# A decoder layer on one core: weight splits on GpSimd, fewer indexer columns, a fixed order in the merge, and the overflow branch at the end

## The chip, the cores and the metric

The kernel runs on one core of a Trainium2 chip. The metric is the device time of one execution in microseconds (us); the median of several executions is compared. The engines are TensorE (PE; its weight loads are PEld), VectorE (DVE), ScalarE (ACT), GpSimd (POOL) and SyncE (SP, which here only issues transfers).

## What is computed

One decoder layer for 512 tokens of width 1024, in float32, and a final RMSNorm:

```python
h = rms_norm(x, g_mix)
qa, ka, va, qb, kb, vb, qi, ki, wi, ga, gb = jnp.split(h @ w_in, SPLIT_POINTS, axis=-1)
qa, ka, qb, kb, qi, ki = (rope(t) for t in (qa, ka, qb, kb, qi, ki))
o_a = moba_attend(qa, ka, va)       # causal blocks
o_b = dsa_attend(qb, kb, vb, qi, ki, wi * IDX_SCALE)   # top 128 keys by the indexer's scores
mixed = sigmoid(ga) * (o_a @ w_proj_a) + sigmoid(gb) * (o_b @ w_proj_b)
x = x + mixed @ w_out
x = x + hier_moe(rms_norm(x, g_ffn), ...)   # top group of 4, top 2 of its 8 SwiGLU experts
return rms_norm(x, g_final)
```

A token attends at most 128 keys in branch B, so the first 128 tokens need no selection and the indexer's scores are only taken for tokens 128 to 511.

## The kernel before

A product of float32 precision is made of three matmuls in a faster type: a matrix is split into a high part (a cast on ScalarE, L172) and a low part (raw minus high, L173, on VectorE or GpSimd), and high times high, high times low and low times high are summed (L266 to L268).

**First part, to about 460 us.** The input projection comes in chunks of 256 columns. SyncE loads each chunk in two halves into one of three buffers `raw`; `halves_of` splits the first half on VectorE and the second on GpSimd into `wh` and `wl`, of which there are two each. `two_blocks` multiplies a chunk in two blocks of 128 columns, 8 steps of 3 matmuls each, over all 512 tokens. `rope_of` rotates on VectorE; `q_stack` and `k_stack` copy the result on ScalarE and take low parts on GpSimd (L319 `qi`, `qa`; L330 `loka`; `kst` is the indexer's key, L384). The indexer's scores (L400 to L404) go into `bias`; the attention quads a0, a1, b0, b1 (scores L443, softmax result `e` L450) are interleaved with the projections by a table of shares (`SHARE`), so that TensorE has other matmuls while a softmax runs. TensorE's instructions are in the order of the program; the other engines are ordered by a scheduler, in which the chunks have a high priority.

**The merge.** For each of 8 blocks of 128 columns TensorE multiplies branch B's output with its projection (12 matmuls, L514 to L516) into one of three PSUM banks `mm`; VectorE multiplies with the gate (L650) and adds branch A (L651); ScalarE writes the high part of the sum for the four token blocks (`mt`, L654), VectorE the low part (L655). The bank is free after that. Between them lie the splits of w_out, three on GpSimd and the last on VectorE. Then x2 = x + mixed W_out (L685 to L689), the norm, the router and a one-hot gather with 32 slots for each expert.

**Second part, from about 480 us.** The 32 experts come in 8 groups of four (`q`), each of 24 pieces of 1 MB that SyncE fetches (L619) into buffers as these come free; TensorE multiplies (L868, L875) and scatters back by a one-hot product into x (L932 to L935). Every token of an expert beyond its 32nd is handled by `rest_of_tokens`, under an If on the largest count. The inputs here have none, so the branch is not entered. The If stands before group 6 (`REST`): eight pieces (`BRIDGE`) are issued by ScalarE ahead of it, then come the load of the count (L1027) and the branch (L1028).

**The tail.** In the last group, for each of 4 token blocks, the first half of x is finished by `combine`, squared on ScalarE (L1088) and multiplied by the norm's weight; then the second half the same way, GpSimd's add and power give the norm's factor (L1105, L1106), the halves are scaled on ScalarE and VectorE (L1107, L1109), and each is sent off by a transfer of 256 KB.

## Time and profile before

| | before |
|---|---|
| median of 3 runs (lowest, highest) | 937.04 us (935.4, 939.02) |
| profiled execution | 939.58 us, its span 937.5 us |
| mean granted clock of TensorE | 0.984 |
| busy: TensorE, VectorE, ScalarE, GpSimd | 93%, 45%, 30%, 19% |

The shares of busy time are averages over two parts of a different kind. The rate of the transfers, slice by slice, tells them apart; then each wait is read in its own stretch: which engine stands, and for whom. The granted clock is given as a share of 2.4 GHz: 1.00 is that, 0.50 is 1.2 GHz.

### The profile page before, as it was taken

How to read it: one execution, taken by the hardware profiler on the slowest of the kernel's cores; microseconds unless marked ns; L12 is line 12 of the kernel's file. 1: busy time of each engine (PE TensorE's matmuls, PEld its weight loads, DVE VectorE, ACT ScalarE, POOL GpSimd, SP SyncE). 2: the span in 40 equal slices, each digit the busy share in tenths (PEclk: the TensorE clock that was granted, in tenths of full speed). 3: DMA queues.
4: the chain of work that ended last, by engine and by line, in shares of the span. 5: the costliest groups of instructions: out<-in, count | busy, mean ns of one | idle time of the engine just before them, and what ended most of it. 6: DMA issues, size and time to landing. Idle time of an engine off the chain costs nothing. (4 is left out here: it accounts for less than half of the span.)

```text
span 937.5 us, 15635 instructions
## 1 busy us (share of the span) xinstructions
PE 875.8 (93%) x6436; PEld 518.0 (55%) x6436; DVE 426.5 (45%) x981; ACT 278.5 (30%) x585; POOL 178.6 (19%) x115
## 2 busy tenths in 40 slices
PE   7999989989999999899999999999998989599885
PEld 5897769768777877689834343422423223133221
DVE  3747899998545554641722323231421302313114
ACT  4546654553443554533510100010100100001013
POOL 1494335243114820600300000000000000000003
PEclk9999999999999999899999999999999999799998
DMA  8422112112214221574589999999999999989995
GB/s 324 153 81 68 46 46 91 45 45 91 68 68 180 90 91 50 188 289 180 208 359 420 420 420 421 420 419 420 419 421 420 421 420 419 417 330 418 422 419 201
DMA packets 41261, 244.49 MB, mean 261 GB/s; under 512 B 4961, under 2 KB 5345, under 8 KB 16609
## 3 DMA queue, kind: packets, MB, share of 16 engines
...
## 5 line engine op out<-in xcount | busy, mean ns | idle before, releaser
L868 PE MATMUL h<-we,xs 128*32 128x512 f32 x2048 | 237.4, 600 | 25.9 <-DMA we<-in_w_e_dram 16.7
L868 PEld LDWEIGHTS h<-we,xs 128*32 128x32 f32 x2048 | 59.0, 110 | 179.3 <-issue 111.9
L875 PE MATMUL y<-we,hT 128*32 128x512 f32 x1024 | 116.1, 595 | 3.0 <-DMA we<-in_w_e_dram 3.0
L266 PE MATMUL mm<-xh,wh 128*128 128x512 f32 x272 | 110.2, 405 | 0.8 <-DVE bias L404 0.8
L268 PE MATMUL mm<-xh,wl 128*128 128x512 f32 x272 | 107.7, 396 | 0.0
L267 PE MATMUL mm<-xl,wh 128*128 128x512 f32 x272 | 107.7, 396 | 0.0
L173 POOL TENSOR_TENSOR wl<-raw,wh 128x1024 fp32r<-128x1024 f32 (+1 forms) x23 | 64.4, 2801 | 135.0 <-ACT wh L172 76.9
L1094 POOL TENSOR_TENSOR fo<-x,gfn 128x512 f32<-128x512 f32 x4 | 5.0, 1272 | 446.4 <-DVE x L935 446.4
L935 DVE TENSOR_TENSOR x<-cps,x 128x512 f32<-128x512 f32 x64 | 43.3, 688 | 82.0 <-PE cps L933 81.9
L875 PEld LDWEIGHTS y<-we,hT 128*32 128x32 f32 x1024 | 30.1, 109 | 74.5 <-issue 56.7
L909 DVE SCALAR_TENSOR_TENSOR silu<-silu,gate,h 128x512 f32<-128x512 f32 x16 | 12.0, 748 | 114.7 <-PE h L868 113.7
L268 PEld LDWEIGHTS mm<-xh,wl 128*128 128x128 f32 x272 | 51.2, 188 | 12.4
L266 PEld LDWEIGHTS mm<-xh,wh 128*128 128x128 f32 x272 | 51.4, 189 | 11.8 <-issue 1.2
L267 PEld LDWEIGHTS mm<-xl,wh 128*128 128x128 f32 x272 | 51.3, 189 | 9.6
L172 ACT CAST wh<-raw 128x1024 fp32r<-128x1024 f32 (+1 forms) x46 | 45.6, 1028 | 32.2 <-DMA raw<-in_w_ch_dram 13.2
L903 ACT ACTIVATE silu<-h 128x512 f32<-128x512 f32 x16 | 9.6, 598 | 146.7 <-PE h L868 119.2
L172 ACT CAST y<-y 128x512 fp32r<-128x512 f32 x32 | 18.7, 586 | 113.6 <-PE y L875 113.6
L916 ACT COPY hT<-htr 128x512 f32<-128x512 f32 x16 | 8.7, 588 | 147.3 <-PE htr L914 147.3
L173 DVE TENSOR_TENSOR y<-y,y 128x512 fp32r<-128x512 f32 x32 | 22.0, 688 | 54.3 <-ACT y L172 54.3
L448 ACT ACTIVATE ps<-e,st 128x128 f32<-128x128 f32 (+3 forms) x64 | 33.5, 524 | 43.7 <-DVE st L447 43.5
L173 DVE TENSOR_TENSOR wl<-raw,wh 128x1024 fp32r<-128x1024 f32 (+1 forms) x23 | 31.9, 1386 | 27.2 <-ACT wh L172 22.6
L687 PE MATMUL mm<-woh,mt 128*128 128x256 f32 x128 | 36.5, 285 | 1.2 <-DVE mt L655 1.2
(201 smaller groups left out, 1569.2 us busy)
## 6 DMA issues: line engine op xcount, KB each, us to landing
we<-in_w_e_dram SPq DMA_DIRECT2D x184, 1024.0 KB, 19.8
...
```

The source lines that it names most:

```text
L172: act.copy(hi, raw)
L173: eng.tensor_tensor(lo, raw, hi.bitcast(F32), ALU.subtract)
L266: pe.matmul(ps, a, xk(k, 0), start=k == 0, stop=False)
L267: pe.matmul(ps, a, xk(k, 1), start=False, stop=False)
L268: pe.matmul(ps, lo[:, k, col:col + P], xk(k, 0), start=False, stop=k == NK - 1)
L448: act.activation(ps[:, :n], e[:, :n], AF.Exp, bias=st[:, 0:1], scale=-1.0, accum_out=st[:, 1:2])
L687: pe.matmul(ps, mt[t][:, 1, k], hi[:, k], start=False, stop=k == NK - 1)
L868: pe.matmul(ps[h][CAP * e:CAP * (e + 1)], xs[:, k, h, CAP * e:CAP * (e + 1)], w[:, e * FF:(e + 1) * FF], start=k == 0, stop=k == NK - 1)
L875: pe.matmul(ys[h][CAP * e:CAP * (e + 1)], hT[h][:, k, CAP * e:CAP * (e + 1)], w[:, e * FF:(e + 1) * FF], start=k == 0, stop=k == 3)
L903: act.activation(out[h], h1[h], AF.Silu)
L909: dve.scalar_tensor_tensor(a[h], a[h], gate[:, h:h + 1], h3[h], ALU.mult, ALU.mult)
L935: dve.tensor_tensor(o, ps, o, ALU.add)
```

## The change

It has five pieces.

1. `halves_of` takes the engine of each half as an argument. All chunks have both halves split on GpSimd, except `qi0` (both on VectorE); the chunks that are loaded ahead of the stream keep the old pair. Of branch B's projection, pieces 2 and 3 are split on GpSimd.
2. The indexer's query chunks `qi0` and `qi1` are projected, rotated and stacked for the tokens 128 to 511 only.
3. In the merge, ScalarE and VectorE follow the order of the program, and the low parts of a block are written after the two operations of the next block.
4. `REST`, `BRIDGE` and the reserve of buffers are gone. All pieces are fetched by SyncE; the count is loaded at q = 1, and the If comes after the output's transfers. If it is entered, the output is computed and written again.
5. The tail follows the order of the program on ScalarE, VectorE and GpSimd. The second half of x is added to the last sums in PSUM by a matmul with the identity (`with_x`), ahead of the last pieces. Squares and norm weights read PSUM; a row of 1024 is scaled at once; four transfers of 512 KB in place of eight. The last group's `selT` and parts have buffers of their own.

```diff
-    def halves_of(hi, lo, src, place=None):
+    def halves_of(hi, lo, src, place=None, engs=(dve, pool)):
...
+            split(hi[:, a:a + 4], lo[:, a:a + 4], raw, engs[a // 4])
             yield
...

-    def proj_T(w, col, ps, ks=range(NK)):
+    def proj_T(w, col, ps, ks=range(NK), t0=0):

         hi, lo = w
         for k in ks:
-            a = hi[:, k, col:col + P]
-            pe.matmul(ps, a, xk(k, 0), start=k == 0, stop=False)
-            pe.matmul(ps, a, xk(k, 1), start=False, stop=False)
-            pe.matmul(ps, lo[:, k, col:col + P], xk(k, 0), start=False, stop=k == NK - 1)
-            yield 0.64
+            a, xhi, xlo, o = hi[:, k, col:col + P], xk(k, 0)[:, t0:], xk(k, 1)[:, t0:], ps[:, t0:]
+            pe.matmul(o, a, xhi, start=k == 0, stop=False)
+            pe.matmul(o, a, xlo, start=False, stop=False)
+            pe.matmul(o, lo[:, k, col:col + P], xhi, start=False, stop=k == NK - 1)
+            yield 0.64 * (T - t0) / T

     done, due = set(), [0.0]
...
         with tc.high_priority(PRIO):
-            return load_split(w_ch[CHUNKS.index(name)])
+            return load_split(w_ch[CHUNKS.index(name)], engs=(dve, dve) if name == "qi0" else (pool, pool))
+
+    def first_token(name):
+
+        return P if name[:2] == "qi" else 0

     def two_blocks(name):
         w, ps = chunk(name), []
         for b in range(2):
             ps.append(bank())
-            yield from proj_T(w, b * P, ps[b])
+            yield from proj_T(w, b * P, ps[b], t0=first_token(name))
...
         for b in range(2):
-            r = rope_of(ps[b])
+            t0 = first_token(name)
+            r = rope_of(ps[b], t0=t0)
             for j, h, l in ((2 * b, LOW, UPP), (2 * b + 1, UPP, LOW)):
-                act.copy(qs[h, j], r[h])
-                pool.tensor_tensor(qs[l, j], r[h], qs[h, j].bitcast(F32), ALU.subtract)
+                act.copy(qs[h, j, t0:], r[h, t0:])
+                pool.tensor_tensor(qs[l, j, t0:], r[h, t0:], qs[h, j, t0:].bitcast(F32), ALU.subtract)

     def k_stack(name, ps):
...
-            split(both[:, 0], both[:, 1], raw, dve)
+            split(both[:, 0], both[:, 1], raw, eng)
...
@@ -540,7 +543,7 @@
             wg = chunk(f"gb{n}")
             for b in range(2):
                 gb.append((yield from gate(wg, b)))
-        wbs.extend(branch_w(1, n, "wl" if n < 2 else "wh") for n in range(4))
+        wbs.extend(branch_w(1, n, *(("wl", dve) if n < 2 else ("wh", pool))) for n in range(4))

     def together(g1, g2, share):
...
@@ -634,6 +637,18 @@
     for dst, src in ((br, b_r), (gfk, g_ffnk), (wr, w_r), (tri, const[:, C_COLS["tri"][0]:])):
         sp.dma_start(out=dst, in_=src)
     dve.tensor_scalar(gf8, gfk, 1.0 / H2, None, ALU.mult)
+    merging = ExitStack()
+    for e in (mybir.EngineType.Activation, mybir.EngineType.DVE):
+        merging.enter_context(tc.manual_schedule(engines={e}))
+    merged = []
+
+    def low_parts(n):
+        for c, py in merged[:n]:
+            for t in range(NT):
+                dve.scalar_tensor_tensor(mt[t][:, 1, c], py[:, t * P:(t + 1) * P], 0.5, mt[t][:, 0, c].bitcast(F32),
+                                         ALU.mult, ALU.subtract)
+        del merged[:n]
+
     for n in range(4):
...
             for t in range(NT):
-                mv, h, l = py[:, t * P:(t + 1) * P], mt[t][:, 0, c], mt[t][:, 1, c]
-                act.activation(h, mv, AF.Copy, scale=0.5)
-                dve.scalar_tensor_tensor(l, mv, 0.5, h.bitcast(F32), ALU.mult, ALU.subtract)
+                act.activation(mt[t][:, 0, c], py[:, t * P:(t + 1) * P], AF.Copy, scale=0.5)
+            low_parts(1)
+            merged.append((c, py))
             if c == 0:
...
+    low_parts(1)
     S.free(*oT["b"], *ma)
     ws.append(w_out_split(raws[3], dve))
+    merging.close()
     in_order.close()
...
+    def with_x(ps, t):
+
+        pe.matmul(ps, ident, x2t(t)[:, 512:], start=True, stop=False, skip_group_check=True)
+        return ps

     def rest_of_tokens():

...
-    waiting = []
+    waiting, total = [], {}
     for q in range(NQ):
-        if q == REST:
-            for f in waiting:
-                f()
-            waiting = []
-            kept[0] = 0
-            fetch(BRIDGE, act)
-            bridge.close()
-            in_order.close()
-            ordered.close()
-            rv = nc.values_load(cint[0:1, 0:1], min_val=0, max_val=T)
-            with tc.If(rv > CAP):
-                rest_of_tokens()
-            ordered.enter_context(tc.manual_schedule(engines={mybir.EngineType.SP}))
-            in_order.enter_context(tc.manual_schedule(engines={mybir.EngineType.PE}))
-            fetch(len(S.idle))
-        if q == REST - 1:
-            bridge = ExitStack()
-            bridge.enter_context(tc.manual_schedule(engines={mybir.EngineType.Activation}))
+        if q == 1:
+            over = nc.values_load(cint[0:1, 0:1], min_val=0, max_val=T)
         if q > 0:
             h1 = two(pa, "sc", "h1")
...
+                           S.get([P, T], F32R, "selT") if q == last else None)
         h3 = two(pt_, "tr", "h3")
         for k in range(NK):
-            if q == REST - 1 and k == 2:
-
-                kept[0] = len(S.idle) + BRIDGE + 6
             use(q, NK + k, up, 1, k, range(2), h3, xs)
+            if q == last and k % 2:
+                t, (p, tag) = k // 2, ((pa, "sc"), (pa, "sc"), (pm, "mm"), (pb, "o"))[k // 2]
+                total[t] = with_x(p.tile([P, 512], F32, tag=tag, name="fin"), t)
         hidden(a, h3, gate)
         if q < last:

...
                 gather(xs, sel, 1, b)
-        ys = two(pa, "sc", "y0")
+        ys = two(pt_, "tr", "y0") if q == last else two(pa, "sc", "y0")
         for k in range(4):
             use(q, 2 * NK + k, down, k, ys, hT)
-        y = parts_of(ys)
         if q == last:
             break
+        y = parts_of(ys)
...
+
+    for e in (mybir.EngineType.Activation, mybir.EngineType.DVE, mybir.EngineType.Pool):
+        in_order.enter_context(tc.manual_schedule(engines={e}))
+    fo = [S.get([P, D], F32, "fo") for _ in range(NT)]
+    junk, ylast = S.get([P, NT, 512], F32, "junk"), S.get([P, 2, 2, 512], F32R, "ylast")
+    FIRST, SECOND = slice(0, 512), slice(512, D)
+
+    def square(t, c, v):
+        act.activation(junk[:, t], v, AF.Square, scale=D ** -0.5, accum_out=ssp[:, t, c:c + 1])
+
+    def first_half(t):
+        square(t, 0, x2t(t)[:, FIRST])
+        pool.tensor_tensor(fo[t][:, FIRST], x2t(t)[:, FIRST], gfn[0][:, FIRST], ALU.mult)
+
+    def second_half(v):
+        for t in range(NT):
+            square(t, 1, v[t])
+            dve.tensor_tensor(fo[t][:, SECOND], v[t], gfn[0][:, SECOND], ALU.mult)
+        for t in range(NT):
+            r = ssp[:, t, 2:3]
+            pool.tensor_tensor(r, ssp[:, t, 1:2], ssp[:, t, 0:1], ALU.add)
+            pool.tensor_tensor(r, r, half[:, 0:1], ALU.pow)
+            if t == 1:
+                act.activation(fo[t], fo[t], AF.Copy, scale=r)
+            else:
+                dve.tensor_scalar(fo[t], fo[t], r, None, ALU.mult)
+        for t in (0, 2, 1, 3):
+            sp.dma_start(out=out[t * P:(t + 1) * P], in_=fo[t])
+
+    def eps():
+        dve.tensor_scalar(ssp[:, :, 0:1], ssp[:, :, 0:1], EPS, None, ALU.add)
+
+    y = parts_of(ys)
+    ys = two(pt_, "tr", "y1")
+    for t in range(NT):
+        combine(selT, y, 0, t)
+        first_half(t)
+        if t % 2:
+            use(q, 2 * NK + 4 + t // 2, down, t // 2, ys, hT)
+    for k in range(2, 4):
+        use(q, 2 * NK + 4 + k, down, k, ys, hT)
+    eps()
+    y = parts_of(ys, ylast)
+    for t in range(NT):
+        sl = selT[:, t * P:(t + 1) * P]
+        for part in range(2):
+            pe.matmul(total[t], sl, y[t // 2][:, part], start=False, stop=part == 1, skip_group_check=True)
+    second_half(total)
     in_order.close()
     ordered.close()


-    fo = [S.get([P, D], F32, "fo") for _ in range(NT)]
-
-    def squares(t, c):
-        junk = t2([P, 512], name="junk", tag="hT")
-        act.activation(junk, x2t(t)[:, c * 512:(c + 1) * 512], AF.Square, scale=D ** -0.5, accum_out=ssp[:, t, c:c + 1])
-
-    def first_half(t):
-        combine(selT, y, 0, t)
-        squares(t, 0)
-        dve.tensor_scalar(ssp[:, t, 0:1], ssp[:, t, 0:1], EPS, None, ALU.add)
-        pool.tensor_tensor(fo[t][:, :512], x2t(t)[:, :512], gfn[0][:, :512], ALU.mult)
-
-    ys = two(pt_, "tr", "y1")
-    for k in range(4):
-        use(q, 2 * NK + 4 + k, down, k, ys, hT)
-        first_half(k)
-    y = parts_of(ys)
-    for t in range(NT):
-        combine(selT, y, 1, t)
-        squares(t, 1)
-        r = small([P, 1], "fin")
-        pool.tensor_tensor(r, ssp[:, t, 1:2], ssp[:, t, 0:1], ALU.add)
-        pool.tensor_tensor(r, r, half[:, 0:1], ALU.pow)
-        act.activation(fo[t][:, :512], fo[t][:, :512], AF.Copy, scale=r)
-        sp.dma_start(out=out[t * P:(t + 1) * P, :512], in_=fo[t][:, :512])
-        dve.scalar_tensor_tensor(fo[t][:, 512:], x2t(t)[:, 512:], r, gfn[0][:, 512:], ALU.mult, ALU.mult)
-        sp.dma_start(out=out[t * P:(t + 1) * P, 512:], in_=fo[t][:, 512:])
+    with tc.If(over > CAP):
+        for t in range(NT):
+            combine(selT, y, 1, t)
+        rest_of_tokens()
+        for t in range(NT):
+            first_half(t)
+        eps()
+        second_half([x2t(t)[:, SECOND] for t in range(NT)])

```

What moves, at three places. **GpSimd in the first 90 us** (`wl` is a split of half a chunk, `qa`, `loka`, `kst`, `qi` the low parts of queries and keys), before:

```order
L173 TENSOR_TENSOR wl<-raw,wh 128x1024 x2
L319 TENSOR_TENSOR qa_12_313<-r,qa_12_313 64x512 x4
L330 TENSOR_TENSOR loka_14_335<-r,hika_13_334 64x512 x8
L173 TENSOR_TENSOR wl<-raw,wh 128x1024
L384 TENSOR_TENSOR kst_364<-r,kst_364 64x512 x2
L173 TENSOR_TENSOR wl<-raw,wh 128x1024
L319 TENSOR_TENSOR qi_19_690<-r,qi_19_690 64x512 x2
L173 TENSOR_TENSOR wl<-raw,wh 128x1024
L319 TENSOR_TENSOR qi_19_690<-r,qi_19_690 64x512 x2
L319 TENSOR_TENSOR qi_20_891<-r,qi_20_891 64x512 x2
```

and after:

```order
L170 TENSOR_TENSOR wl<-raw,wh 128x1024 x4
L322 TENSOR_TENSOR qa_12_313<-r,qa_12_313 64x512 x4
L333 TENSOR_TENSOR loka_14_335<-r,hika_13_334 64x512 x8
L387 TENSOR_TENSOR kst_364<-r,kst_364 64x512 x2
L170 TENSOR_TENSOR wl<-raw,wh 128x1024 x2
L322 TENSOR_TENSOR qi_19_672<-r,qi_19_672 64x384 x2
L170 TENSOR_TENSOR wl<-raw,wh 128x1024 x2
L322 TENSOR_TENSOR qi_19_672<-r,qi_19_672 64x384 x2
L322 TENSOR_TENSOR qi_20_838<-r,qi_20_838 64x384 x2
L170 TENSOR_TENSOR wl<-raw,wh 128x1024 x2
```

Where one split, a chunk's second half, stood, there are two; the one of qi0's second half, which stood ahead of `kst`, is gone; the indexer's low parts have 384 columns.

**VectorE in the merge** (`mm` is a PSUM bank, `g` a gate, `ma` branch A's result, `mt` a low part), before:

```order
L655 SCALAR_TENSOR_TENSOR mt_3597<-mm,mt_3597 128x128 x2
L650 SCALAR_TENSOR_TENSOR mm<-g,mm 128x512
L655 SCALAR_TENSOR_TENSOR mt_3598<-mm,mt_3598 128x128
L651 TENSOR_TENSOR mm<-ma_2260,mm 128x512
L655 SCALAR_TENSOR_TENSOR mt_3598<-mm,mt_3598 128x128
L655 SCALAR_TENSOR_TENSOR mt_3599<-mm,mt_3599 128x128
L655 SCALAR_TENSOR_TENSOR mt_3596<-mm,mt_3596 128x128
L655 SCALAR_TENSOR_TENSOR mt_3599<-mm,mt_3599 128x128
L655 SCALAR_TENSOR_TENSOR mt_3597<-mm,mt_3597 128x128
L655 SCALAR_TENSOR_TENSOR mt_3598<-mm,mt_3598 128x128
L655 SCALAR_TENSOR_TENSOR mt_3599<-mm,mt_3599 128x128
```

and after:

```order
L665 SCALAR_TENSOR_TENSOR mm<-g,mm 128x512
L666 TENSOR_TENSOR mm<-ma_2260,mm 128x512
L665 SCALAR_TENSOR_TENSOR mm<-g,mm 128x512
L666 TENSOR_TENSOR mm<-ma_2260,mm 128x512
L648 SCALAR_TENSOR_TENSOR mt_3596<-mm,mt_3596 128x128
L648 SCALAR_TENSOR_TENSOR mt_3597<-mm,mt_3597 128x128
L648 SCALAR_TENSOR_TENSOR mt_3598<-mm,mt_3598 128x128
L648 SCALAR_TENSOR_TENSOR mt_3599<-mm,mt_3599 128x128
L665 SCALAR_TENSOR_TENSOR mm<-g,mm 128x512
L666 TENSOR_TENSOR mm<-ma_2260,mm 128x512
```

The gate and the sum of the next block stood between low parts of one block, or behind them; now the pair comes first and four low parts of the block before it follow.

**SyncE at the branch**, before, in front of group 6:

```order
L619 DMA we_6819<-in_w_e_dram 128x2048
L619 DMA we_6829<-in_w_e_dram 128x2048
L1028 COMPARE_AND_BRANCH
L946 COMPARE_AND_BRANCH
L946 UNCONDITIONAL_BRANCH x2
L1160 BRANCH_PREFETCH_HINT
```

and after, at the end of the program (`fo` is an output row block):

```order
L622 DMA we_7588<-in_w_e_dram 128x2048
L622 DMA we_7598<-in_w_e_dram 128x2048
L1114 DMA out_dram<-fo_7753 128x1024
L1114 DMA out_dram<-fo_7755 128x1024
L1114 DMA out_dram<-fo_7754 128x1024
L1114 DMA out_dram<-fo_7756 128x1024
L1139 COMPARE_AND_BRANCH
L968 COMPARE_AND_BRANCH
```

The branch stood between two pieces of the stream; now all pieces and the output stand ahead of it.

## Rows read from the trace of the kernel before

**Rows 1.** The page: rate in 40 slices; the chain that ended last, by line.

```profile
GB/s 324 153 81 68 46 46 91 45 45 91 68 68 180 90 91 50 188 289 180 208 359 420 420 420 421 420 419 420 419 421 420 421 420 419 417 330 418 422 419 201
DMA we<-in_w_e_dram 9%; PE y L875 1%; ACT junk L1088 0%; POOL fin L1106 0%; PE h L868 0%; POOLq L1160 0%; PE cps L932 0%; DVE fo L1109 0%; POOL fin L1105 0%; PE gtr L885 0%; SPq L619 0%; ACT y L172 0%; PE cps L933 0%; ACT fo L1107 0%; DVE ssp L1093 0%
```

**Rows 2.** Stretches: start:end, length, busy PE, PEld, DVE, ACT, POOL, clock, DMA share, GB/s.

```profile
180.00:200.00 20.00, 16.38 (x96) 12.25 (x95) 19.53 (x51) 9.88 (x23) 7.52 (x5) 1.00 0.15 53
480.00:500.00 20.00, 20.00 (x204) 7.94 (x195) 4.17 (x6) 1.12 (x3) 0.00 (x0) 1.00 1.01 422
820.00:840.00 20.00, 20.00 (x188) 6.00 (x184) 1.29 (x2) 1.20 (x2) 0.00 (x0) 1.00 0.76 310
```

**Rows 3.** TensorE's waits, 76 to 205 us: total us, times, longest.

```profile
PE ps L443 <- DVE e L450: 5.4, 4, 2.1
PE ips L400 <- DVE bias L404: 3.0, 5, 1.3
PE mm L266 <- DVE bias L404: 0.8, 1, 0.8
```

**Rows 4.** Groups of VectorE, 76 to 200: splits, busy us, mean ns, idle.

```profile
L173 DVE TENSOR_TENSOR wl<-raw,wh 128x1024 fp32r<-128x1024 f32 x7 | 11.1, 1586 | 0.0
```

**Rows 5.** Line L173: count, ns lowest/median/highest, first and last start.

```profile
L173 DVE TENSOR_TENSOR wl<-raw,wh x23: 692/1224/2995, 4.5 to 342.8; 128x1024 fp32r<-128x1024 f32 x22, 128x512 fp32r<-128x512 f32 x1
L173 POOL TENSOR_TENSOR wl<-raw,wh x23: 1804/2492/3457, 12.4 to 343.8; 128x1024 fp32r<-128x1024 f32 x22, 128x512 fp32r<-128x512 f32 x1
```

**Rows 6.** Timeline of TensorE, projection of ka0: start us, length.

```profile
27.31 0.39 PE L266 MATMUL ps_k<-xh,wh 128*128 128x512 f32 x1
32.68 0.40 PE L268 MATMUL ps_k<-xh,wl 128*128 128x512 f32 x1
```

**Rows 7.** Timeline of GpSimd, 41 to 74 us.

```profile
41.55 3.36 POOL L173 TENSOR_TENSOR wl<-raw,wh 128x1024 fp32r<-128x1024 f32 x1 [9.22 <-ACT wh L172]
50.46 11.63 POOL L330 TENSOR_TENSOR loka<-r,hika 64x512 fp32r<-64x512 f32 x8
64.52 3.64 POOL L384 TENSOR_TENSOR kst<-r,kst 64x512 fp32r<-64x512 f32 x2
71.36 2.65 POOL L319 TENSOR_TENSOR qi<-r,qi 64x512 fp32r<-64x512 f32 x2 [0.71 <-POOL wl L173]
```

**Rows 8.** Timeline of TensorE: the first score with qi0's second block.

```profile
81.81 0.36 PE L400 MATMUL ips<-kst,qi 128*128 128x256 f32 x1
```

**Rows 9.** Timeline of TensorE, the two waits of the merge.

```profile
387.02 0.80 PE L514 MATMUL mm<-oh,wab 128*128 128x512 f32 x1 [2.93 <-DVE mt L655]
408.11 0.38 PE L687 MATMUL mm<-woh,mt 128*128 128x256 f32 x1 [1.25 <-DVE mt L655]
```

**Rows 10.** The stretch behind the first of them, as rows 2.

```profile
388.00:392.00 4.00, 4.00 (x11) 3.09 (x10) 1.12 (x5) 0.83 (x3) 3.92 (x3) 0.50 0.00 0
```

**Rows 11.** Groups of VectorE in the merge, 384 to 412 us.

```profile
L655 DVE SCALAR_TENSOR_TENSOR mt<-mm,mt 128x128 fp32r<-128x128 f32 x30 | 8.0, 288 | 4.2 <-ACT mt L654 3.4
L650 DVE SCALAR_TENSOR_TENSOR mm<-g,mm 128x512 f32<-128x512 f32 x6 | 4.2, 694 | 4.1 <-PE mm L516 4.1
```

**Rows 12.** The branch's own line, L1028: what TensorE's sequencer shows.

```profile
L1028 PEldq COMPARE_BRANCH  x1: 6426/6426/6426, 802.9 to 802.9; - x1
```

**Rows 13.** What SyncE waits for in the whole run.

```profile
SPq L1028 <- SPq L1028: 39.3, 1, 39.3
```

**Rows 14.** The tail: last piece in the chain; timelines of ScalarE, GpSimd, SyncE.

```profile
903.72 18.27 DMA we<-in_w_e_dram
...
924.31 0.63 ACT L1088 ACTIVATE junk<-x 128x512 f32<-128x512 f32 x1
925.55 0.57 ACT L172 CAST y<-y 128x512 fp32r<-128x512 f32 x1
...
928.47 0.95 POOL L1106 TENSOR_TENSOR fin<-fin,half 128x1 f32<-128x1 f32 x1
...
929.01 0.35 SPq L1108 DMA_DIRECT2D out_dram<-fo  x1
```

44 lines of the change are left out of this document (21 added, 23 removed).

## Prediction, made before the changed kernel was run

> **What bounds the kernel now.** I read the page's rate line and the chain that ended last first, then stretches of 20 us, then what the engines wait for. The rate line shows two programs in one [rows 1]: up to about 460 us the transfers are far below what they reach later, and from 500 us on every slice but two reads 417 to 422 GB/s. The chain consists of expert weights, 9%, and of little else [rows 1]. In the stretch 480 to 500 the DMA engines are full, share 1.01 at 422 GB/s [rows 2]. So the second part is a fixed volume at a fixed rate: its end moves with its start, with every hole in the stream, and with what follows the last piece. Its start is set by the first part, since the pieces go into buffers that the first part frees; 1 us there is 1 us at the end.
>
> In the first part TensorE sets the pace, with one soft place. In 180 to 200 TensorE is busy 16.38 us and VectorE 19.53 of 20 [rows 2], and between 76 and 205 us TensorE waits for VectorE 5.4 us before the attention scores, 3.0 before the indexer scores and 0.8 before a projection [rows 3]: 9.2 us. In the merge it waits 2.93 and 1.25 us, again for VectorE [rows 9].
>
> **The sum is made against the profiled execution, 939.58 us** (span 937.5); the median of the runs is 937.04, so 2.5 is taken off at the end. The measurement can tell about 0.5%, 4.7 us.
>
> **1. 384 columns in the indexer queries.** Four blocks of 24 matmuls go from 512 to 384 columns. In the projection of ka0, 23 steps of 512 columns lie between 27.31 and 32.68 [rows 6]: 0.2335 us each. A quarter is 0.058, times 96 is 5.6 us of TensorE work. The two rope passes lose a quarter as well, 16 VectorE instructions of about 0.69 each (a 128x512 from PSUM takes 0.694 [rows 11]), 2.8 us, partly ahead of the soft place; two low parts on GpSimd go from 2.65 [rows 7] to an estimated 2.0.
>
> **2. Splits on GpSimd.** It takes the first half of every chunk but qi0 from VectorE and gives it to GpSimd, ahead of the second half in the same queue. Gain: between 76 and 200 us VectorE runs seven such splits, 11.1 us [rows 4]. Cost: a split lasts 2.49 us on GpSimd by the median against 1.22 on VectorE [rows 5], and the pair now comes in series, 5 to 6.9 us, where it came side by side. While TensorE has the chunk before to work on (48 steps of 0.2335, 11.2 us) this is hidden. It is not hidden at the start, where GpSimd is a chain: before, it ended the second split of va1 at 44.9, ran qa's low parts, ka's (8 in 11.63 us), then kst's 3.64, and the first low parts of qi0 only at 71.36 [rows 7]. After, by the new order: va1's first half goes ahead as well, +2.5; one half of qi0 is gone, -2.4; kst ends at about 67.5, qi1 both halves 72.5, qi0 first block 74.5, qa1 both halves 79.5, qi0 second block 81.5. TensorE needs that last one for the first score that now stands at 81.81 [rows 8]; with 2.8 us saved on qi0 and about 1 on qi1 it would be there at 78. So it waits some 3.3, and of the 5.6 of part 1 stay 2.3 (bounds: 0 if GpSimd's neighbours slow its splits to the maximum 3.46 [rows 5], 5.6 if the splits start early). Against that stands the relief of VectorE: 11.1 us off, where 9.2 us are waited for. Not all of what it ran lies ahead of a wait; I take somewhat over half of the 9.2, 5.2 (bounds 2 and 9). **Parts 1 and 2: 7.5 us, between 2 and 14.** Later chunks (the gates) alternate with the other branch's product on TensorE, and two splits in series fit into a chunk's 11.2 us. The two splits of branch B's projection that go to GpSimd stand before its w_out splits, which is an engine with slack there.
>
> A split on either engine is slow when the other runs one: on VectorE 1.22 by the median and 2.99 at most, on GpSimd 2.49 and 3.46 [rows 5]. The Trainium skill, SBUF — State Buffer, section "Who interferes with whom", says that a VectorE instruction with two SBUF inputs and a GpSimd instruction that reads SBUF exclude each other, and that one with a single SBUF input does not; the spread of these rows agrees. By that rule the moved splits would meet few rivals on VectorE, whose scores and rope read PSUM as one input, and the chain above would stand at the medians; without it, at the maxima, four splits of the chain would end it some 4 us later and nothing of the 5.6 would stay.
>
> **3. The merge in program order.** Before, the low parts of a block, each waiting for its cast, sit on VectorE between the two operations that free the next bank. TensorE waits 2.93 us at 387.02 [rows 9], and after that pause runs at 1.2 GHz: granted clock 0.50 in 388 to 392 [rows 10]. Its 14 matmuls to 392.7 come 0.425 apart, not 0.2335: 2.7 us more. A last wait of 1.25 stands at 408.11 [rows 9]. Together 6.9. After, VectorE's row is two operations of 0.69, L650's and its twin L651's, and four low parts of 0.29 [rows 11], and the low parts belong to a block whose casts are long done: 2.5 us a block, below TensorE's 12 steps, 2.8. A bank comes free just in time, so I leave 0.9 of waits. **6.0 us, between 4 and 7.** What is late next is the last block's low parts, ahead of the last w_out split; the split is needed only from the third column block on.
>
> **4. The branch in the middle.** At its If, SyncE waited 39.3 us for all transfers in flight [rows 13], since a join lets no queue run on, and the eight pieces that ScalarE issued ahead did not cover it. In 820 to 840 the stream reads 310 GB/s against 422 [rows 2]: 20 x (1 - 310/420) = 5.2 us lost. TensorE stood too, its jump lasting 6426 ns [rows 12], but behind it the transfers went on, so only the hole counts. With the If at the end, SyncE issues the pieces throughout, and the hole has nothing left to come from. **5.2 us, between 4 and 5.5.**
>
> **5. The tail.** Before, from the last piece (903.72 + 18.27 = 921.99) to 937.5 are 15.5 us [rows 14]. The second cast of the last product starts only at 925.55, behind squares on ScalarE, and the first output leaves at 929.01 [rows 14], eight of them in turn. After: product 1.1 us, two casts of 0.57 [rows 14] and two low parts of about 0.69, the last 8 matmuls: sums ready 3.0 to 4.4 after the piece. Four squares of 0.63 [rows 14], now from PSUM, then GpSimd's add and power, 0.95 a time [rows 14], one after the other, against four multiplications and three whole-row scalings on VectorE: first row at 6.6, last at about 9. 2.1 MB at 420 GB/s are 5.0, at the tail's lower rate 5.5; with 0.9 to the first byte the data end at 13, and 1.4 more closes the program as now: 14.4. The If stands after the output's issue. Its jumps on TensorE and ScalarE lie beside the 5 us of output; I put 0.5 on it. **0.6 us, between -2 and 1.2.** A row's output waits for both halves now, which is why this is small although 4 transfers replace 8.
>
> **Sum:** 7.5 + 6.0 + 5.2 + 0.6 = 19.3; 939.6 - 19.3 = 920.3, less 2.5: **917.7 us**, chance 0.60, its own range 911 to 923.
>
> **Rivals.** (a) *GpSimd takes the first part back:* TensorE waits for low parts and pairs of splits about as long as it waited for VectorE; term 1+2 is 0 to 2. For it: the chain above has no slack to 81 us. The Trainium skill, GPSIMD Engine Reference, section 4.1 "Engine selection", would have it so: elementwise work on two tiles belongs on VectorE, GpSimd being about twice as slow; by the medians of [rows 5], 2.49 to 1.22, each chunk's weights come about 2.5 us later, and the rule would give this rival's time. Against it: later GpSimd has room, 7.5 of 20 us busy in 180 to 200 [rows 2]. 924; chance 0.17. (b) *The jump at the end is exposed:* the engine that ends last pays what TensorE paid, 6.4 us [rows 12]: 924. Against: TensorE's last matmul ends some 9 us before the output does, and its jump lies in that time. The Trainium skill, Runtime: NRT & Kernel Launch, section "Instruction fetch mechanics", says that a taken branch outside the fetched window must fetch its target by a transfer first; by it each engine pays here, and SyncE, which jumps last, would give this rival's time; the row of TensorE agrees, the rows of the others are not shown. Chance 0.07. (c) *VectorE's waits vanish wholly* and the chain has slack: term 1+2 is 13 or more: 911; chance 0.07. (d) *Slower:* the pairs stand behind the key stacks' low parts. 8 of these last 11.63, two splits up to 6.9, together 18.5 against the 11.2 us of a chunk: 7.3 us of wait at each of ka1, kb0, kb1, and about 1 at each of three query chunks; 25 us. Then term 1+2 is 5.6 - 25 = -19.4 in place of 7.5, 917.7 + 26.9 = 945. It decides from about 23 us of such waits on. Against: the new order has the first split pair of a chunk between the two blocks of the stacks, not behind all eight. Chance 0.05. (e) *It doesn't do what it says:* the merge's bank and the hole stay, because the stream was late for another reason: 930 to 937, chance 0.04.
>
> **Range.** All lower bounds together give 939.6 - 8 - 2.5 = 929, all upper ones 939.6 - 27.7 - 2.5 = 909; with (a) and (b) inside, **908 to 930**. Faster by over 0.5% (below 932.4): 0.60 + 0.17 + 0.07 + 0.07 = 0.91, less 0.03 for mishaps of two terms at once: 0.88. Slower by over 0.5%: 0.05 of (d) and 0.01. Same: 0.06.
>
> **What would show it.** Rate of 417 or more in every slice from 500 us to the end of the stream; no clock of 0.50 near 390 and no wait over 1 us in the merge; TensorE waiting for GpSimd's qi near 78 to 82 for about 3 us, and the waits for VectorE halved; last landing to end about 15. A later start of the stream than some 13 us earlier than now would prove terms 1 to 3 wrong.

## The result

| | before | changed |
|---|---|---|
| median (lowest, highest) | 938.03 us (935.4, 939.53), 4 runs | 922.48 us (922.03, 923.14), 4 runs |
| profiled execution | 939.58 us, span 937.5 | 922.07 us, span 920.3 |
| mean granted clock | 0.984 | 0.995 |

The ratio is 0.9838, 95% interval 0.982 to 0.9855: 15.6 us faster. The prediction said 917.7 with a range of 908 to 930. The direction and the range held; the forecast gain was too large by about a quarter, and the terms under it are further off than their sum, since one of them errs the other way.

The two profiled executions are 17.5 us apart. Four points that both programs pass, the landmarks of what follows, split this (the starts of the same matmuls on TensorE's timeline, and the last landing in the chain):

| stretch | before | changed | gain |
|---|---|---|---|
| to the third column block of the merge (its first matmul) | 381.13 | 373.30 | 7.8 |
| from there to the first expert matmul | 84.56 | 77.08 | 7.5 |
| from there to the last piece's landing | 456.30 | 453.14 | 3.2 |
| from there to the span's end | 15.5 | 16.8 | -1.3 |

The rest, 0.3, lies outside the span. **The rate line of the page**, changed kernel, answers to [rows 1]: from 500 us on no slice but the last lies under 416, and the slice at 330 is gone.

```profile
GB/s 326 149 72 104 61 21 92 70 46 69 84 66 195 69 92 67 196 365 94 320 374 420 420 420 420 420 419 421 418 421 419 421 420 421 421 419 420 421 416 140
```

**What TensorE waits for between 62 and 205 us**, changed kernel (us in total, times, longest), answers to [rows 3]. The longest four are shown. The waits for the softmax's `e` fall from 5.4 to 1.7, but a wait for GpSimd's `qi`, predicted at 3.3, stands at 2.6, and there are waits for ScalarE's `pt` and others that were in no row of before.

```profile
PE ips L403 <- POOL qi L322: 2.6, 1, 2.6
PE ps L446 <- DVE e L453: 1.7, 2, 1.3
PE ops L474 <- ACT pt L464: 1.3, 3, 0.6
PE ips L403 <- DVE r L294: 0.6, 1, 0.6
```

**Stretches of the changed kernel** (columns as in [rows 2]). In 180 to 200 VectorE is full, 20.00 of 20; relieving it did not leave it idle, it let TensorE come sooner. The second row is the merge, where [rows 10] had a clock of 0.50: TensorE is busy throughout at 1.00.

```profile
180.00:200.00 20.00, 18.50 (x107) 13.77 (x107) 20.00 (x57) 13.42 (x30) 10.62 (x8) 1.00 0.17 54
380.00:384.00 4.00, 4.00 (x18) 3.21 (x18) 3.38 (x11) 3.31 (x10) 3.23 (x2) 1.00 0.94 324
```

**The end of the stream**, changed kernel, us by us. The rate falls from 352 in the first of these to nothing behind the last, over 7 us.

```profile
896.00:897.00 1.00, 0.76 (x8) 0.34 (x12) 0.91 (x2) 0.65 (x3) 0.60 (x1) 1.00 0.85 352
...
899.00:900.00 1.00, 1.00 (x10) 0.29 (x12) 1.00 (x2) 0.41 (x1) 0.37 (x1) 1.00 0.49 205
...
902.00:903.00 1.00, 1.00 (x12) 0.11 (x4) 0.19 (x1) 0.00 (x0) 0.16 (x1) 1.00 0.20 82
```

In the kernel before, the same end takes 2 us; a decline like that of the changed kernel stood there in front of the stop in the middle, over 5 us from 821 on (the last three rows):

```profile
919.00:920.00 1.00, 0.54 (x8) 0.16 (x8) 0.00 (x0) 0.00 (x0) 0.80 (x1) 1.00 0.97 401
920.00:921.00 1.00, 1.00 (x16) 0.26 (x8) 0.00 (x0) 0.00 (x0) 0.00 (x0) 1.00 0.34 139
921.00:922.00 1.00, 0.49 (x8) 0.00 (x0) 0.00 (x0) 0.00 (x0) 0.00 (x0) 1.00 0.10 41
...
821.00:822.00 1.00, 1.00 (x16) 0.28 (x12) 0.00 (x0) 0.00 (x0) 0.00 (x0) 1.00 0.79 328
...
825.00:826.00 1.00, 1.00 (x12) 0.24 (x8) 0.00 (x0) 0.00 (x0) 0.00 (x0) 1.00 0.34 139
826.00:827.00 1.00, 1.00 (x16) 0.31 (x12) 0.00 (x0) 0.00 (x0) 0.00 (x0) 1.00 0.00 0
```

**The tail**, changed kernel: the last piece in the chain (landing at 903.52), the output's issue on SyncE's timeline, the last stretches with output in them, and what SyncE shows at the new branch. Answers to [rows 13, 14]. By the packets in the trace the output's last bytes arrive at 917.75, 14.2 us after the landing, as before (936.17 less 921.99), but SyncE still stands behind its jump until 918.9, and the span ends 2.5 us after the data, where it was 1.3.

```profile
884.95 18.57 DMA we<-in_w_e_dram
...
910.54 3.21 SPq L1114 DMA_DIRECT2D out_dram<-fo  x4
...
916.00:917.00 1.00, 0.00 (x0) 0.00 (x0) 0.00 (x0) 0.00 (x0) 0.00 (x0) 0.50 0.90 356
917.50:917.75 0.25, 0.00 (x0) 0.00 (x0) 0.00 (x0) 0.00 (x0) 0.00 (x0) 0.50 0.04 16
...
L1139 SPq COMPARE_BRANCH  x1: 45/45/45, 913.8 to 913.8; - x1
L1139 SPq EVENT_SEMAPHORE  x8: 17/17/17, 918.2 to 918.9; - x8
```

### The profile page after: what moved, and what is told of

It reads as the page before. It is cut to its first block, busy times and chain, and to the rows that moved or that the text cites. A ratio compares the mean times of both kernels' runs of the same rounds, so it can differ in the third digit from the quotient of the medians.

```text
span 920.3 us, 15647 instructions
## 1 busy us (share of the span) xinstructions
PE 870.0 (95%) x6444; PEld 513.7 (56%) x6444; DVE 400.5 (44%) x957; ACT 273.1 (30%) x582; POOL 210.4 (23%) x135
## 4 chain that ended last, share of the span: by engine, by line
PE 59%; DMA 30%; DVE 5%; POOL 2%; ACT 2%; issue 1%; SPq 0%; POOLq 0%; ACTq 0%
DMA we<-in_w_e_dram 28%; PE h L885 9%; PE y L892 7%; PE mm L263 5%; PE mm L265 5%; PE mm L264 5%; PE ops L474 2%; PE mm L703 2%; PE mm L702 2%; PE mm L704 2%; PE mm L518 2%; PE mm L519 2%; PE mm L517 2%; PE mm L348 2%; PE mm L350 2%; PE mm L349 2%
## 5 line engine op out<-in xcount | busy, mean ns | idle before, releaser
L170 POOL TENSOR_TENSOR wl<-raw,wh 128x1024 fp32r<-128x1024 f32 (+1 forms) x41 | 97.1, 2389 | 110.1 <-ACT wh L169 54.5
L263 PE MATMUL mm<-xh,wh 128*128 128x512 f32 (+1 forms) x272 | 108.8, 400 | 0.7 <-DVE bias L407 0.5
L265 PE MATMUL mm<-xh,wl 128*128 128x512 f32 (+1 forms) x272 | 105.8, 389 | 0.5 <-DVE wl L170 0.5
L264 PE MATMUL mm<-xl,wh 128*128 128x512 f32 (+1 forms) x272 | 105.4, 387 | 0.0
L952 DVE TENSOR_TENSOR x<-cps,x 128x512 f32<-128x512 f32 x60 | 41.1, 688 | 92.6 <-PE cps L950 92.4
L704 PE MATMUL mm<-woh,mt 128*128 128x256 f32 x128 | 36.9, 289 | 0.0
L702 PE MATMUL mm<-woh,mt 128*128 128x256 f32 x128 | 36.6, 286 | 0.0
```

Of the source, the lines that this page charges most:

```text
L170: eng.tensor_tensor(lo, raw, hi.bitcast(F32), ALU.subtract)
L263: pe.matmul(o, a, xhi, start=k == 0, stop=False)
L264: pe.matmul(o, a, xlo, start=False, stop=False)
L265: pe.matmul(o, lo[:, k, col:col + P], xhi, start=False, stop=k == NK - 1)
L702: pe.matmul(ps, a, hi[:, k], start=k == 0, stop=False)
L704: pe.matmul(ps, mt[t][:, 1, k], hi[:, k], start=False, stop=k == NK - 1)
```

## The experiments

All compare by medians with the kernel before, run beside them on the same chip (937.0 to 937.9 us there; 938.7 beside the two single executions); the ratios are against that. The changed kernel stands at 922.5 and was not run again beside them. Since the kernel before moves by about 1 us between chips, a difference of under 1 us from 922.5 is not told from none.

**The first two pieces, undone one at a time and together.** All tokens again in the indexer queries:

```diff
-        return P if name[:2] == "qi" else 0
+        return 0
```

> The changed kernel (922.5 us), but with the indexer queries projected, rotated and stacked for all 512 tokens again. Theory 'parts add': TensorE gets 5.6 us of work back, and its wait of 2.6 us for GpSimd's low parts of qi goes, since it comes there 3.8 us later; the first part ends 3 us later and the kernel takes 925 to 926. Rival 'VectorE limits': between 120 and 200 us VectorE is full whatever TensorE saved before, so what the 384 columns save is waited away there: 922 to 923.

Measured: 923.17 us (922.86 to 923.41), 0.9849 of before (0.9831 to 0.9867). The rival holds: the 384 columns are worth 0.7 us here, which is not clear of none. TensorE has its 5.6 us of work again, and stands nearly as much less: the wait for `qi` went from 2.6 to 0.5, and those for `pt` and `r` shrank too. TensorE's time beyond 0.2335 us for 512 columns, added up from the starts between 62 and 215 us, is 20.7 us in the changed kernel and 15.8 here, 4.9 less.

```profile
PE ps L446 <- DVE e L453: 1.4, 1, 1.4
PE ips L403 <- POOL qi L322: 0.5, 1, 0.5
```

The old splits:

```diff
-            return load_split(w_ch[CHUNKS.index(name)], engs=(dve, dve) if name == "qi0" else (pool, pool))
+            return load_split(w_ch[CHUNKS.index(name)], engs=(dve, pool))
...
-        wbs.extend(branch_w(1, n, *(("wl", dve) if n < 2 else ("wh", pool))) for n in range(4))
+        wbs.extend(branch_w(1, n, *(("wl", dve) if n < 2 else ("wh", dve))) for n in range(4))
```

> The changed kernel (922.5 us), but with the splits shared as before (first half VectorE, second half GpSimd, branch B's pieces all on VectorE). Theory 'parts add': TensorE's waits for VectorE up to 205 us go from 3.3 us back to about 10, the 2.6 us for GpSimd's qi go to nothing: 926 to 927. Rival 'GpSimd's chain ate it': the two cancel, 921 to 923.

Measured: 933.60 us (928.82 to 935.16), 0.9943 (0.9922 to 0.9965): 11.1 us lost, more than either theory. The waits for VectorE between 62 and 205 us come to 12.1 us, 2 more than expected:

```profile
PE ps L446 <- DVE e L453: 4.3, 3, 2.6
PE ips L403 <- DVE r L294: 3.3, 1, 3.3
PE mm L263 <- DVE bias L407: 2.5, 2, 1.8
PE ips L403 <- DVE bias L407: 2.0, 2, 1.6
```

They do not make 11 by themselves (waits of all kinds between 62 and 205 us: 12.6 here, 7.2 in the changed kernel, 5.4 apart). Most of the rest is TensorE's clock: after three of these waits it runs at 1.2 GHz for some us. In stretches of 5 us:

```profile
90.00:95.00 5.00, 2.66 (x10) 2.23 (x11) 4.81 (x12) 3.34 (x9) 1.64 (x2) 0.81 0.56 197
125.00:130.00 5.00, 3.74 (x13) 3.08 (x14) 5.00 (x15) 1.25 (x4) 0.00 (x0) 0.72 0.00 0
190.00:195.00 5.00, 2.54 (x7) 2.18 (x8) 4.94 (x17) 2.57 (x7) 2.08 (x2) 0.71 0.64 210
```

Summed over such stretches to 215 us the missing share of the clock is 5.15 us, the most that the drops can have cost. In the profiled execution of the changed kernel every stretch of 20 us up to 220 has 1.00.

Both undone, by the two edits above together:

> The changed kernel (922.5 us) with both of the first two pieces undone: splits shared as before and all 512 tokens in the indexer queries; merge, branch and tail stay changed. Theory 'VectorE limits': alone, the 384 columns put TensorE ahead of VectorE and cost more waits and more time at 1.2 GHz than they save, so undoing both costs only what the first part gained against before, 7.8 us: 930, less than the 933.6 of undoing the splits alone. Rival 'parts add': 384 columns are worth some 1 us in either setting: 934 to 935.

Measured: 925.97 us (925.52 to 927.05), 0.9878 (0.9864 to 0.9892). The sign that the first theory asked for is there, and stronger than its number: with the old splits the 384 columns cost 7.6 us (933.6 against 926.0), with the new ones they save 0.7. TensorE, ahead by 5.6, runs into a VectorE that is not. And the two pieces together are worth 3.5 us, not the 7.8 between the two profiled executions. The other 4.3 lie between this kernel's first part, which has the same order on every engine as that of before, and that of before. Three executions with the first part of before have a profile: the kernel before itself and the two versions of it without the branch further down. From TensorE's 40th projection step (at about 62 us) to the third column block of the merge:

| execution | us | clock of 0.50 on the way |
|---|---|---|
| kernel before | 319.1 | behind the wait at 157 us |
| before without the If | 317.6 | none |
| before with a plain stream | 318.4 | at 193 us |
| both pieces undone | 315.5 | none |
| changed kernel | 310.7 | none |

So 0.8 of the 4.3 us lie ahead of 62 us, where executions of one program differ, and about 1.5 are the clock's fall in one execution. The other 2.1 are in all three executions of before: a wait of 1.81 us for the softmax that the one execution with both pieces undone does not have. The wait comes from who is first at 151 us, a split on VectorE or one on GpSimd. In this kernel VectorE starts 0.11 us ahead and takes 1.22 us, and GpSimd 3.37:

```profile
151.41 1.22 DVE L170 TENSOR_TENSOR wl<-raw,wh 128x1024 fp32r<-128x1024 f32 x1
...
151.52 3.37 POOL L170 TENSOR_TENSOR wl<-raw,wh 128x1024 fp32r<-128x1024 f32 x1 [0.94 <-ACT wh L169]
```

In the kernel before GpSimd is ahead by 0.49 us and takes 2.40, VectorE 3.00, and TensorE waits 1.81 us for the softmax behind it:

```profile
151.89 2.40 POOL L173 TENSOR_TENSOR wl<-raw,wh 128x1024 fp32r<-128x1024 f32 x1 [0.36 <-POOL loka L330]
...
152.38 3.00 DVE L173 TENSOR_TENSOR wl<-raw,wh 128x1024 fp32r<-128x1024 f32 x1
...
156.89 0.35 PE L443 MATMUL ps<-hika,qa 128*128 128x256 f32 x1 [1.81 <-DVE e L450]
```

The two versions without the branch show the same (GpSimd ahead by 0.52 and 0.53, VectorE 2.97 and 2.96, the wait 1.81 and 1.82), so it belongs to the program of before; why GpSimd comes first there and not here is open. The Trainium skill, SBUF — State Buffer, section "Who interferes with whom", says that the order of issue decides who blocks. The two pairs of rows agree, and the one that comes second is late by about what is left of the other's instruction. The changed kernel has no split on VectorE at this place; its longest split on GpSimd is 2.52 us, where [rows 5] had 3.46.

The new splits also cost something, ahead of 62 us. At 28 us VectorE scales four small tiles (`dg`) that TensorE needs next. One such instruction takes 0.27 us, and 2.42 where a split on GpSimd lies beside it. In the changed kernel two splits stand there in series, in the kernel with the old splits one (nanoseconds, lowest/median/highest):

```profile
L369 DVE TENSOR_SCALAR dg<-cb,rstd x4: 274/1346/2416, 28.4 to 33.3; 128x128 f32<-128x128 f32 x4
...
L369 DVE TENSOR_SCALAR dg<-cb,rstd x4: 273/276/2425, 28.8 to 31.6; 128x128 f32<-128x128 f32 x4
```

TensorE waits 0.8 us for them there. From its 16th to its 32nd projection step, with this inside, it takes 13.0 us in all seven profiled executions with the new splits and 12.0 in all seven with the old ones. So the two pieces gain 4.8 us behind 62 us (315.5 less 310.7) and lose 1.0 here.

**Does the clock's fall explain the spread?** The eight runs with the old splits lie at 928.8 to 930.0 (three) and 933.0 to 935.2 (five).

> The same kernel as with the old splits, once more with a profile; its runs lie in two groups, 929 to 930 and 933 to 935, and the profile taken was of 934.2 with three drops of TensorE's clock in the first 200 us. Theory 'the clock falls or not': the waits are the same to 0.5 us in every execution, and the time follows the number of drops: near 934 three drops, near 929 one or none. Rival 'the waits differ': three drops or none, an execution near 929 has some 4 us less of waits.

> As the run before this one: the same kernel a third time with a profile, to have one of each group. Theory 'the clock falls or not': waits the same to 0.5 us, time by the number of drops. Rival 'the waits differ': some 4 us less of waits near 929.

Measured: 932.03 and 931.13, with the profile. The waits are the same in all three executions to 0.1 us a row; in the second, for example:

```profile
PE ps L446 <- DVE e L453: 4.3, 3, 2.6
```

The clock is not: at the same three places the second execution has 1.00, 0.80 and 0.50, the third 0.66, 0.66 and 1.00.

```profile
90.00:95.00 5.00, 4.18 (x25) 3.17 (x25) 4.04 (x10) 3.75 (x10) 2.03 (x2) 1.00 0.61 213
125.00:130.00 5.00, 5.00 (x25) 3.73 (x24) 3.80 (x11) 1.21 (x3) 0.00 (x0) 0.80 0.00 0
190.00:195.00 5.00, 5.00 (x14) 3.88 (x14) 4.03 (x12) 2.07 (x7) 2.32 (x2) 0.50 0.32 129
```

```profile
90.00:95.00 5.00, 3.91 (x12) 3.21 (x13) 3.55 (x11) 3.42 (x10) 1.99 (x2) 0.66 0.61 213
125.00:130.00 5.00, 5.00 (x17) 4.04 (x18) 4.25 (x12) 1.33 (x3) 0.00 (x0) 0.66 0.00 0
190.00:195.00 5.00, 3.84 (x19) 3.15 (x19) 4.94 (x17) 2.96 (x8) 2.58 (x2) 1.00 0.63 205
```

So the wait is given by the program, and whether the clock falls behind it is not. Nor does the number of drops give the time: the drop at 188 us of the second execution lasts twice as long as each of the others, so that it has as much time at 1.2 GHz as the first with its three. From the 40th projection step to the first expert matmul the three take 399.2, 398.9 and 398.2 us; up to that step 62.7, 61.2 and 61.3. The third, with one drop less, is 1.0 us ahead of the first in this stretch, and 1.4 of the difference of 3.1 comes from the first 62 us. No execution near 929 was caught, so what makes those stays open.

**The merge.** Undone by leaving out the two `manual_schedule` lines and writing each low part behind its high part, as before:

```diff
-                act.activation(mt[t][:, 0, c], py[:, t * P:(t + 1) * P], AF.Copy, scale=0.5)
-            low_parts(1)
-            merged.append((c, py))
+                mv, h, l = py[:, t * P:(t + 1) * P], mt[t][:, 0, c], mt[t][:, 1, c]
+                act.activation(h, mv, AF.Copy, scale=0.5)
+                dve.scalar_tensor_tensor(l, mv, 0.5, h.bitcast(F32), ALU.mult, ALU.subtract)
```

> The changed kernel (922.5 us), but with ScalarE and VectorE ordered by the scheduler in the merge, low parts of a block directly behind its high parts. Theory 'parts add': the merge's waits and the stretch at 1.2 GHz come back whole, 7.6 us: 930. Rival 'state on entry': the waits of before came from where the splits of branch B's projection stood on VectorE, and two of these are on GpSimd now; then 3 to 5 us come back: 926 to 927.

Measured: 928.63 us (927.86 to 930.18), 0.9909 (0.9893 to 0.9924): 6.1 us, between the two. The waits are back, 0.82, 2.40 and 1.25 us on TensorE's timeline, but this time the clock did not fall behind them:

```profile
375.82 0.50 PE L519 MATMUL mm<-oh,wab 128*128 128x512 f32 x1 [0.82 <-DVE wab L170]
380.81 0.50 PE L517 MATMUL mm<-oh,wab 128*128 128x512 f32 x1 [2.40 <-DVE mt L668]
399.21 0.38 PE L701 MATMUL mm<-woh,mt 128*128 128x256 f32 x1 [1.25 <-DVE mt L668]
```

```profile
380.00:384.00 4.00, 3.19 (x14) 2.61 (x15) 2.21 (x9) 2.24 (x7) 3.92 (x3) 1.00 0.00 0
```

From the third column block to the third output step this execution takes 28.5 us, the changed kernel 22.6, and the kernel before 30.7 with the drop of [rows 10]. So the order is worth 6.0 up to there without a drop of the clock, of which the three waits make 4.5 (the 0.82 is for a split of branch B's weights that comes late on VectorE here), and up to the first expert matmul 5.4. Up to that matmul the kernel before loses 7.5, 2 more, with its drop. That drop stands in all three profiled executions with the merge of before, here in the plain stream:

```profile
385.00:389.00 4.00, 3.42 (x8) 2.77 (x9) 1.85 (x7) 2.29 (x8) 3.92 (x2) 0.50 0.00 0
```

**The branch.** First the stream without anything in the middle. In the kernel before, only the load of the count and the If were taken out; ScalarE's eight pieces stayed:

```diff
-            rv = nc.values_load(cint[0:1, 0:1], min_val=0, max_val=T)
-            with tc.If(rv > CAP):
-                rest_of_tokens()
```

> The kernel before (938 us) with the load of the count and the If left out (tokens beyond an expert's 32 slots are not handled; the inputs have none). Theory 'drift': without the stop in the middle the 16 transfer engines are no longer brought into line there, drift apart over the whole stream and finish its end one after another over 6 to 7 us, as in the changed kernel: of the hole's 5.35 us only 3.1 are gained, 935. Rival 'hole alone': the end of the stream is as steep as now, 2 us, and 5.3 us are gained: 932.5.

Measured: 945.18 us (942.45 to 946.11), 1.0080 (1.0063 to 1.0097): slower, and no answer to the question. Without the join SyncE goes on issuing while ScalarE issues its eight pieces, over 31.6 us instead of 11.6; pieces of one group now come through two queues, and TensorE waits 19.3 us, at eight places, for the one it needs next.

```profile
801.84 31.55 ACTq L619 DMA_DIRECT2D we<-in_w_e_dram  x8
...
PE h L868 <- DMA we<-in_w_e_dram: 19.3, 8, 4.9
```

So the cleaner version: the count, the If, and ScalarE's pieces all out, all 192 pieces on SyncE.

```diff
-        if q == REST:
...
-            fetch(BRIDGE, act)
...
-            rv = nc.values_load(cint[0:1, 0:1], min_val=0, max_val=T)
-            with tc.If(rv > CAP):
-                rest_of_tokens()
...
-            if q == REST - 1 and k == 2:
-
-                kept[0] = len(S.idle) + BRIDGE + 6
```

> The kernel before (938 us) with the load of the count, the If, and ScalarE's eight pieces left out: SyncE issues all 192 pieces in their order, and nothing stops in the middle (tokens beyond an expert's 32 slots are not handled). Theory 'drift': the 16 transfer engines are no longer brought into line in the middle and finish the stream's end one after another over 6 to 7 us as in the changed kernel; from the first expert matmul to the last landing 453.2 us in place of 456.3, 935. Rival 'hole alone': the end stays as steep as in before, 2 us, 451.0 us, 932.5.

Measured: 933.89 us (932.13 to 935.74), 0.9956 (0.994 to 0.9972): 4.0 us. From the first expert matmul (464.25) to the last landing (917.26) it takes 453.0 us, as the first theory said. The time alone does not decide between the two theories: three of the six runs lie at 932.1 to 932.8, with a mean clock of 0.994 to 0.996, and three at 935.0 to 935.7, with 0.991, among them the profiled one. The stretch and the shape of the end do. The hole is gone, and the end falls off over 7 us as in the changed kernel:

```profile
820.00:840.00 20.00, 16.16 (x154) 5.60 (x154) 2.88 (x4) 0.31 (x1) 0.00 (x0) 1.00 1.01 420
...
911.00:912.00 1.00, 1.00 (x12) 0.26 (x8) 0.84 (x2) 0.00 (x0) 1.00 (x2) 1.00 0.67 279
...
915.00:916.00 1.00, 1.00 (x12) 0.26 (x8) 0.00 (x0) 0.00 (x0) 0.18 (x1) 1.00 0.33 139
```

The hole's 5.3 us are all found in the stream: the bytes moved by 840 us, counted from the same point, are 2.25 MB ahead in the changed kernel, 5.35 us at 420 GB/s. Then 2.2 of them go at the end. The hole in the kernel before had two parts: the decline from 821 to 826 us costs 2.1 us of full rate, the empty time behind it 3.2. Taking the stop out gained the empty time; the decline only moved to the end of the stream. All thirteen profiled executions without the stop end over 6 to 7 us. With it, the stream falls off over 5 us in front of the stop and over 2 us at its end, 93 us of transfers later. That the transfer engines run apart over a long stream, and that the stop brought them into line, is an inference from these shapes; the trace does not tell the 16 engines apart, so which of them lag is open.

Then the branch at the end, left out of the changed kernel together with the load of its count:

```diff
-        if q == 1:
-            over = nc.values_load(cint[0:1, 0:1], min_val=0, max_val=T)
...
-    with tc.If(over > CAP):
-        for t in range(NT):
-            combine(selT, y, 1, t)
...
```

> The changed kernel (922.5 us) with the load of the count and the If left out (tokens beyond an expert's 32 slots are not handled; the inputs have none). Theory 'the join is exposed': SyncE's waits behind its jump, 4.3 us, end 1.8 us later than the end of the data would allow, as the stretch from the end of the data to the end of the program is 3.2 us against 1.4 before: 920.7. Rival 'the end waits for the output anyway': 922.5.

Measured: 921.22 us (920.96 to 922.41), 0.9826 (0.9814 to 0.9839): 1.3 us, against 1.8 expected (which took the data to end at 917.1, where the rate had fallen to a tenth; the last bytes come at 917.75). From the last landing (904.46) to the span's end (919.0) are 14.5 us, against 16.8, so in the profiled executions the branch costs 2.3 behind the landing: 1.0 while the output is moved (its last bytes arrive 13.2 us after the landing here and 14.2 there) and 1.2 behind the data. The 0.9 by which the landing itself is later here is in the first part, where this execution's clock is at 0.50 behind the wait for `qi`.

**A version beyond both.** If GpSimd's chain and VectorE's load both hold TensorE up, relieving one alone should do little. First the chain, with the weights of qi1 on VectorE too:

```diff
-engs=(dve, dve) if name == "qi0" else (pool, pool)
+engs=(dve, dve) if name in ("qi0", "qi1") else (pool, pool)
```

> The changed kernel (922.5 us) with the weights of qi1 split on VectorE too, so that GpSimd's low parts of qi0 come 4.7 us earlier. Theory 'GpSimd's chain': TensorE's wait of 2.6 us for qi goes and stays gone: 920. Rival 'VectorE limits': TensorE waits that much longer for VectorE behind it, which is full between 120 and 200 us: 922 to 923.

Measured: 921.92 us (920.81 to 923.04), 0.9835 (0.9822 to 0.9847); 0.6 us, so the rival is nearer, though 0.6 is not told from none. The wait for `qi` went to 1.4 only. Then VectorE's load:

```diff
-                dve.tensor_scalar(e[:, :n], ps[:, :n], st[:, 2:3], None, ALU.mult)
+                if br == "a" and s == 1:
+                    act.activation(e[:, :n], ps[:, :n], AF.Copy, scale=st[:, 2:3])
+                else:
+                    dve.tensor_scalar(e[:, :n], ps[:, :n], st[:, 2:3], None, ALU.mult)
```

> The changed kernel (922.5 us) with every second scaling of the softmax in branch A's quads (16 of 32, 0.29 to 0.75 us each, 8 us in all) on ScalarE in place of VectorE. Theory 'VectorE limits the stretch to 200 us': ScalarE has room there (9 to 13 of 20 us busy), TensorE's waits for VectorE (1.7, 0.5, 0.5, 0.6) shrink: 919 to 921. Rival 'the chain limits': TensorE waits for the length of the chain score, exponential, scaling, transpose, not for a full engine; one more change of engine in it makes that no shorter: 922 to 924.

Measured: 921.73 us (921.54 to 922.55), 0.9836 (0.9814 to 0.9859): 0.8 us, again not told from none. And both edits:

> Both at once: every second scaling of branch A's softmax on ScalarE, and the weights of qi1 split on VectorE (922.5 us without, 921.9 with the second alone). Theory 'VectorE limits': with VectorE relieved, GpSimd's wait of 2.6 us can be taken away for good: 918. Rival 'the chain limits': 921 to 923.

Measured: 919.93 us (919.0 to 922.5), 0.9824 (0.9799 to 0.9849). It is 2.5 us under the changed kernel by the medians, half of what the first theory said, but only 1.3 by the ratios against the kernel before, whose intervals overlap, and the highest of its runs reaches the changed kernel's. Nor is it shown that the two edits are worth more together than apart. From the 40th projection step to the third column block the changed kernel takes 310.7 us, the first edit 309.5, the second 310.8 and both 308.0. The execution of the second has a drop of the clock behind the wait for `qi` at 79 us; two other executions with the unedited first part and such a drop, those with the old merge and without the branch, take 312.0 and 312.3. So the first is worth 1.2, the second 1.2 to 1.5 and both 2.7: they add. The same stretch in the second edit's execution and in the changed kernel's:

```profile
80.00:83.00 3.00, 3.00 (x13) 3.00 (x12) 1.53 (x6) 1.46 (x4) 2.02 (x2) 0.50 0.24 87
...
80.00:83.00 3.00, 3.00 (x21) 3.00 (x20) 1.82 (x7) 2.42 (x7) 2.47 (x3) 1.00 0.35 127
```

With both edits, TensorE's waits for the two causes, and the new one for ScalarE:

```profile
PE ips L403 <- POOL qi L322: 1.4, 1, 1.4
PE ps L446 <- ACT e L454: 0.8, 1, 0.8
```

## Why the prediction was right or wrong

**What bounds the kernel: right.** The stream starts as much earlier as the first part ends earlier (15.3 us at the first expert matmul), and all that is gained ahead of it arrives.

**Parts 1 and 2, 7.5 us (2 to 14): the step that failed is the sum of two terms that do not add.** The prediction took 2.3 for the columns and 5.2 for VectorE's relief. The mechanisms were there in the trace: 5.6 us less work on TensorE, a wait of 2.6 for `qi` (3.3 predicted), waits for VectorE down from 10.0 in all to 3.3. But a saving ahead of a full engine is waited away behind it: the columns are worth 0.7 with the new splits and -7.6 with the old ones, the splits 11.1 with the short columns and 2.8 with the long. Together they are worth 3.5 by the medians, inside the bounds and half the value taken, or 5.6 against executions of before with the wait at 156 us and no drop of the clock behind it (3.5 and 2.1). The 7.8 between the two profiled executions agree with the 7.5 by luck: they hold the slow start and the drop of one execution. Rival (a) put this at 0 to 2.

**The split's price: right in kind.** GpSimd's pairs take 4.7 to 4.8 us, the medians of [rows 5], not the maxima; the chain ended at 80.4, by the prediction at 81.5. What the prediction did not count is the 1.0 us at 28 to 33 us, where a moved split does meet VectorE.

**Part 3, 6.0 us (4 to 7): the mechanism right, the size too small.** Undone in the changed kernel it is worth 6.1 by the median, 5.4 to the first expert matmul in a stretch without a drop; between the two profiled executions it is 7.5, above the upper bound. The prediction counted 4.2 in waits and 2.7 for the clock, less 0.9 for waits that would stay. None stayed. The clock's share is there in all three profiled executions of before's merge, and not in the one with the old merge in the changed kernel; the higher mean clock of three other runs of the plain stream suggests that it is not in every execution of before either.

**Part 4, 5.2 us: the hole was sized rightly and given back in part.** "The hole has nothing left to come from" holds. What the prediction did not see is that 2.1 of the hole's 5.3 us were the decline of the rate in front of the stop, and not the stop: without the stop it comes at the end of the stream, 2.2 us. By landmarks 3.2 remain, by the run without a branch 4.0.

**Part 5, 0.6 us (-2 to 1.2): the sign was wrong, the bound held.** The step that failed is the 0.5 put on the If. Without it the tail takes 14.5 us where before had 15.5, so the tail's own gain of 1.0 is what the prediction had without that 0.5 (1.1). The branch costs 2.3 by landmarks and 1.3 by medians: 1.2 us are SyncE's join behind the jump, and 1.0 us the output takes longer beside the branch, for a cause that stays open. TensorE's jump took 3371 ns, from 906.9 to 910.3, and ended before the output's first issue at 910.54; the jumps of the other engines took 45 to 72 ns, so rival (b) fell with its price of 6.4.

**The step from the profiled execution to the median, -2.5: right in size.** The profiled execution of before was slow by its start (it reached the 40th projection step at 62.0 us, the two versions without the branch at 60.8 and 61.1) and by the drop of the clock at 157 us, 1.5. Against an execution without these two the gains are 5.6, 7.5, 3.2 and -1.3, in sum 15.0, near the 15.6 of the medians. The forecast had 7.5, 6.0, 5.2 and 0.6: errors of +1.9, -1.5, +2.0 and +1.9 us, 4.3 in all, of the 4.8 by which 917.7 fell short of 922.5. The measured time lies inside the forecast's own narrow range, 911 to 923, only because the merge was worth 1.5 more than was taken.
